# Attention operands and value differences kept in DRAM as high and low parts, and a head's two half results stored apart, in a decoder block

## The chip, the cores and the metric

The kernel runs on one core of a Trainium2 chip. The metric is the device time of one execution in microseconds (us); less is better. The times before are of three runs, and one more execution was profiled.

## The reference, cut to what matters

A decoder block over 1024 rows of 1024 values in float32: a norm, one wide input projection, two mixers side by side (stick-breaking attention of 8 heads of 64, and a gated linear attention, GLA, of 4 heads), each with its own projection and gate, an output projection, and a gated feed-forward part with a convolution of width 3 (2816 channels).

```python
proj = xn @ w_in      # sb q,k,v | GLA q,k,v,r,a | two gates
z = einsum('bhqd,bhkd->bhqk', qb, kb) * scale
log_keep = where(strict, log_sigmoid(-z), 0.0)
tail = cumsum(log_keep, reverse=True) - log_keep
w = where(strict, exp(log_sigmoid(z) + tail), 0.0)
o_sb = einsum('bhqk,bhkd->bhqd', w, vb)
y = sigmoid(gate_sb + b0) * (o_sb @ w_branch_sb) + sigmoid(gate_gla + b1) * (o_gla @ w_branch_gla)
h = h + y @ w_out
h = h + conv_ffn(rms_norm(h), ...)
```

## The kernel before, in words

Every matrix product is made of fp32r operands: a float32 value is split into a high part (a cast on ScalarE, ACT) and a low part (a subtraction on VectorE, DVE), and `mac` (L196) adds three products, high by high, high by low and low by high. So TensorE (PE) is fed by splits: `split` is a cast (L119) and a subtraction (L110). All products of the two big projections go through an Strassen-like scheme (`fast` steps), whose operands are sums of quarters.

The program runs through these stages:

- 0 to 114 us: norm, transposes, and the value projections. The last of these (`value`, L367) makes the GLA values, in a loop of 8 steps (i). In the same loop `sums` makes sums of the quarters on DVE (L110, L116) with their splits, and `differences(i)` subtracts each value row from the one before it: two loads (L439, L444), a POOL subtraction (L445), a POOL-issued store of 256 KB to `dv_d` (L446).
- 114 to 316 us: ten pairs of `fast` products (L196), some 20 us of PE each. `project_pairs` loads weights (L172, 2 loads of 512 KB a pair on the queue of SyncE, SP), splits them and adds the results on DVE (L116). `keep` finishes a pair: the eight tiles of attention queries and keys (128x1024) are stored to `sqk_d` from the POOL queue (L535).
- 316 to 545 us: attention, `attend`: four head pairs j, in each four steps tp and two heads e. `weigh` makes scores (L664), a sigmoid on ACT (L666), a mask on POOL (`affine_select`, L668) and a scan on DVE (L671). `turn_weights` transposes (L678) and splits, `gather` multiplies with the value differences (L687), whose stationary tile holds high and low part side by side (`vt`, 128 columns), so that the result has two halves of 64 partitions: ACT takes the lower one with a bias (L692), DVE adds the upper one (L116, 64x256), and SP stores 64 KB to `osb_d` (L695). `weigh` runs ahead of `gather` by up to six chunks (`AHEAD`) or 12 blocks. Between, `fill(gate_steps, 1)` puts products of the gates (L196, L568) on PE.
- `keys(j)` loads three pieces for each of two halves (256 KB each, L584, L586, SP) and splits them (ACT L590, DVE L110 64x1024), `queries(j, th)` loads two (L599) and splits them (ACT L602, DVE L110 128x1024), `value_blocks` loads 256 KB of `dv_d` for each block (L653) and splits it, `whole21` loads a quarter of the input back (`x21_d`, in rows `x_d`; L610, two loads of 1 MB) and rounds it with four casts (L614). All these loads are on SP. Their instructions are set between the chunks by generators (`coming`, `again`).
- 545 to 618 us: GLA (`gated`, L781 to L854) with the first branch projection: `osb_d` is loaded back in eight tiles of 128x512 (L955), each split by L119 and L110, and multiplied by `w_branch_sb`. The order in which `first_branch` and `gated` alternate is set by the counters `GLA`.
- 618 to 1411 us: second branch, output projection, the feed-forward part. The diff touches nothing here.

Tiles come from rings: `t8` 16 buffers, `t4` 14, `t2` 11, PSUM banks 8. A load whose buffer is still read waits in its queue, and so does all that stands behind it in that queue. The order of instructions on each engine is that of the recorded program.

Of the kernel before, what the change touches and what calls it, by code (L numbers as in the profile page):

```python
# [17 lines left out]
P = 128  # L18
# [27 lines left out]
EVERY = 1  # L46
# [19 lines left out]
def block_kernel(ctx: ExitStack, tc: tile.TileContext, x, norm_mix_g, w_in, b_gate, w_alpha_up, b_alpha,  # L66
# [32 lines left out]
    def dram(name, rows, cols):  # L99
        return dp.tile([rows, cols], F32, tag=name, name=name)  # L100
# [55 lines left out]
    dv_d = dram("dv_d", S, SBH * SBD)  # L156
    sqk_d, gr_d = dram("sqk_d", 2 * SBH * SBD, S), dram("gr_d", GH * GV, S)
    qd_d, ki_d, kt_d = (dram(n, GH * GK, S) for n in ("qd_d", "ki_d", "kt_d"))
    gate_d, ga_d = dram("gate_d", 2 * D, S), dram("ga_d", 2 * RANK, S)
    osb_d = dram("osb_d", SBH * SBD, S)  # L160
    x21_d = dram("x21_d", 2 * P, 2 * D)
# [270 lines left out]
    for n, v in enumerate(xq["21"]):  # L432
        nc.gpsimd.dma_start(by(x21_d[n * P:(n + 1) * P, :], 4), v.bitcast(F32))

    def differences(i):
# [10 lines left out]
        nc.gpsimd.dma_start(dv_d[rows, :], a)  # L446

    xsums = sums(xq)
    for i in range(NT):
        differences(i)  # L450
        fill(xsums, 2)
        value(ws2, (i + 4) % NT, gv_d)
# [68 lines left out]
    def keep(pair):  # L521
        def finish(*os):
# [3 lines left out]
            for o, (_, dst, r0) in zip(os, pair):  # L526
# [4 lines left out]
                if dst is gate_d:  # L531
# [46 lines left out]
    def keys(j, t):  # L578

        kk, raw = by(t8(), 2), t4()  # L580
# [12 lines left out]

    def queries(j, th, t):
# [687 lines left out]
```

## Time and profile before

| | |
|---|---|
| time, median of 3 runs (least to greatest) | 1412.22 us (1410.84 to 1413.24) |
| profiled execution: its own time | 1412.8 us |
| its span, granted TensorE clock | 1411.1 us, 0.994 |
| PE busy | 1385.3 us (98%) |
| PE weight load busy | 1145.4 us (81%) |
| DVE busy | 1065.4 us (76%) |
| ACT busy | 650.4 us (46%) |
| POOL busy | 111.5 us (8%) |
| bytes moved by DMA | 216.87 MB, 153 GB/s over the span |

In the rows further down, a time stands in microseconds from the start of the span, and "a<-b" is a tile written from a tile read. "x12" after a row is the number of instructions in it; a bracket behind a timeline row is the idle time of that engine before it and what ended it. A granted clock (PEclk) of 1.00 is TensorE's upper level (2.4 GHz), 0.5 its lower (1.2 GHz).

### The profile page before, as it was taken

What the parts mean: (1) busy time and instruction counts of PE and PEld (TensorE: products, weight loads), DVE (VectorE), ACT (ScalarE), POOL (GpSimd) and SP (SyncE); (2) the same over time, 40 slices, a digit from 0 to 9 for tenths busy, and PEclk for the clock granted to TensorE, in tenths of its full rate; (3) what the DMA queues carried; (4) which work ended last, traced back from release to release, by engine and by line L of the source; (5) the groups of instructions that cost most, each with busy time, mean ns of one, the idle gap of its engine ahead of it and who ended that gap; (6) DMA issues with size and microseconds to landing.
All of it is one profiled execution on the core that took longest, in us unless ns stands there. A gap on an engine that the chain in (4) does not pass through costs nothing.

```text
span 1411.1 us, 18434 instructions
## 1 busy us (share of the span) xinstructions
PE 1385.3 (98%) x6577; PEld 1145.4 (81%) x6577; DVE 1065.4 (76%) x1642; ACT 650.4 (46%) x1246; POOL 111.5 (8%) x198
## 2 busy tenths in 40 slices
PE   7999999999999999999999999999999999999997
PEld 6787888888888888878888788888888888888886
DVE  6398766767888875638446998998888977896765
ACT  6234444647766664543234543333333333454653
POOL 0040000001211110300000000100000000000000
PEclk9999999999999999999999999999999999999999
DMA  6365144276534346465324434564554437953332
GB/s 249 141 203 148 47 142 142 82 211 203 152 94 122 113 150 202 167 224 179 117 93 135 103 107 149 189 209 140 179 179 149 159 106 270 328 163 101 98 106 97
DMA packets 160188, 216.87 MB, mean 154 GB/s; under 512 B 10026, under 2 KB 103276, under 8 KB 159584
## 3 DMA queue, kind: packets, MB, share of 16 engines
q1 hardware_dynamic: 140848, 157.56, 36.5%
q0 software_dynamic: 11952, 43.58, 8.1%
q10 hardware_dynamic: 7296, 14.55, 2.8%
q8 instruction: 52, 0.85, 0.2%
q14 instruction: 40, 0.33, 0.1%
HBM read 155.75 MB, written 59.90 MB: 153 GB/s over the span
## 4 chain that ended last, share of the span: by engine, by line
PE 79%; issue 11%; DVE 6%; DMA 2%; ACT 1%; POOL 1%; POOLq 0%; ACTq 0%; DVEq 0%; SPq 0%
PE bank L196 46%; PE bank L1145 15%; PE bank L1012 5%; PE bank L367 3%; DVE t L110 3%; PE bank L687 2%; DVE t L116 2%; PE bank L664 2%; PE bank L678 2%; PE bank L320 1%; DMA gate_d<-t 1%; PE bank L427 1%; PE bank L818 1%; ACT t L119 0%; PE bank L781 0%
## 5 line engine op out<-in xcount | busy, mean ns | idle before, releaser
L196 PE MATMUL bank<-t,t 128*128 128x512 f32 x3648 | 870.6, 394 | 3.0 <-DVE t L110 2.6
L196 PEld LDWEIGHTS bank<-t,t 128*128 128x128 f32 x3648 | 682.7, 189 | 150.6 <-DVE t L110 3.8
L110 DVE TENSOR_TENSOR t<-t,t 128x512 fp32r<-128x512 f32 (+2 forms) x651 | 430.9, 696 | 82.6 <-ACT t L119 76.0
L119 ACT CAST t<-t 128x512 fp32r<-128x512 f32 x537 | 311.8, 620 | 321.5 <-DVE t L116 74.0
L116 DVE TENSOR_TENSOR t<-bank,t 128x512 f32<-128x512 f32 (+1 forms) x284 | 183.2, 655 | 119.9 <-PE bank L196 65.3
L1145 PE MATMUL bank<-t,t 128*128 128x512 f32 x924 | 209.6, 389 | 0.0
L1145 PEld LDWEIGHTS bank<-t,t 128*128 128x128 f32 x924 | 173.4, 188 | 36.0
L110 DVE TENSOR_TENSOR t<-t 128x512 f32<-128x512 f32 (+1 forms) x124 | 88.4, 721 | 5.6 <-DMA t<-in_w_ffn_in_dram 3.2
L367 PE MATMUL bank<-t,t 128*128 128x512 f32 x384 | 91.9, 398 | 0.0
L110 DVE TENSOR_TENSOR t<-bank,t 128x512 fp32r<-128x512 f32 (+4 forms) x128 | 72.2, 576 | 24.3 <-ACT t L119 23.9
L116 DVE TENSOR_TENSOR t<-t,t 128x512 f32<-128x512 f32 x107 | 76.8, 750 | 16.1 <-ACT t L487 15.4
L1012 PE MATMUL bank<-t,t 128*128 128x512 f32 x384 | 88.9, 391 | 0.0
L1043 ACT ACTIVATE t<-t,vcol 128x1024 f32<-128x1024 f32 x22 | 27.4, 1244 | 127.6 <-DVE t L116 124.0
L367 PEld LDWEIGHTS bank<-t,t 128*128 128x128 f32 x384 | 72.8, 192 | 15.6 <-DVE t L110 0.4
L1012 PEld LDWEIGHTS bank<-t,t 128*128 128x128 f32 x384 | 71.6, 188 | 14.7
L119 ACT CAST t<-bank 128x512 fp32r<-128x512 f32 (+3 forms) x124 | 61.6, 509 | 40.2 <-PE bank L320 19.7
L1045 DVE SCALAR_TENSOR_TENSOR t<-t,vcol,t 128x1023 f32<-128x1023 f32 (+1 forms) x44 | 56.3, 1279 | 14.1 <-ACT t L1043 13.9
L671 DVE TENSOR_TENSOR_SCAN t<-t,zero 128x128 f32<-128x128 f32 (+1 forms) x64 | 52.2, 823 | 16.0 <-POOL t L668 15.5
L664 PE MATMUL bank<-t,t 128*128 128x128 f32 (+3 forms) x192 | 55.5, 368 | 0.4 <-DVE t L110 0.4
L678 PE MATMUL bank<-ident,t 128*128 128x128 f32 x288 | 52.3, 274 | 0.8 <-DVE t L116 0.4
L668 POOL TENSOR_SCALAR_AFFINE_SELECT t<-t 128x128 f32<-128x128 f32 x64 | 33.3, 526 | 212.4 <-ACT t L666 199.2
L666 ACT ACTIVATE t<-bank 128x128 f32<-128x128 f32 (+3 forms) x96 | 45.7, 499 | 6.0 <-PE bank L664 4.3
(127 smaller groups left out, 773.6 us busy)
## 6 DMA issues: line engine op xcount, KB each, us to landing
t<-in_w_ffn_in_dram SPq DMA_DIRECT2D x50, 512.0 KB, 4.2
t<-in_w_in_dram SPq DMA_DIRECT2D x43, 512.0 KB, 5.3
act_d<-t POOLq DMA_DIRECT2D x22, 512.0 KB, 6.0
t<-in_w_ffn_out_dram SPq DMA_DIRECT2D x22, 512.0 KB, 7.5
wsum_d<-t POOLq DMA_DIRECT2D x22, 512.0 KB, 4.1
t<-act_d SPq DMA_DIRECT2D x22, 512.0 KB, 6.1
t<-wsum_d SPq DMA_DIRECT2D x44, 256.0 KB, 3.1
t<-sqk_d SPq DMA_DIRECT2D x40, 256.0 KB, 4.2
```

The costliest lines, as they stand in the source:

```text
L110: nc.vector.tensor_tensor(out=o, in0=a, in1=b, op=ALU.subtract)
L116: nc.vector.tensor_tensor(out=o, in0=a, in1=b, op=ALU.add)
L119: nc.scalar.copy(h, src)
L196: nc.tensor.matmul(pt, a[:, kk], b[:, kk], start=start and kk == 0 and m == 0, stop=stop and kk == k - 1 and m == 2)
L367: nc.tensor.matmul(pt, a[:, k % 4, t], b, start=k == 0 and m == 0, stop=k == NK - 1 and m == 2)
L664: nc.tensor.matmul(z[:, 0:w], q[:, a, e, ts_], kk[:, e, b0 * P:b1 * P], start=a == 0, stop=a == 1)
L666: nc.scalar.activation(ke[:, 0:w], z[:, 0:w], AF.Sigmoid, scale=-SBD ** -0.5)
L671: nc.vector.tensor_tensor_scan(out=kr, data0=kr, data1=zero.to_broadcast([P, w]), initial=1.0 if right is None else right[:, 0:1], op0=ALU ...
L678: nc.tensor.transpose(pt[:, b * P:(b + 1) * P], ke[:, b * P:(b + 1) * P], ident)
L1012: nc.tensor.matmul(pt, a[:, k % 4, t], b, start=(k == 0 and m == 0), stop=(k == NK - 1 and m == 2))
L1045: nc.vector.scalar_tensor_tensor(out=cv[:, i:], in0=av[:, :S - i], scalar=col(V_CW, (2 - i) * NF + f), in1=cv[:, i:], op0=ALU.mult, op1=AL ...
L1145: nc.tensor.matmul(pts[m][i], a[:, t], b, start=(k == 0 and x_ == 0), stop=(k == NH - 1 and x_ == 2))
```

## The change

Queries and keys are split in `keep`, when they are made, and stored as two tensors `sqkh_d` and `sqkl_d`. The value differences are split in `differences`, which moves out of the loop of value products into the loop of the `fast` steps (called at n = 0, and at odd n up to 15, so that block 0 is made twice), and stored 128x1024. Attention then loads finished parts, all from the POOL queue: `keys` four loads of 256 KB, `queries` four of 256 KB, `value_blocks` 512 KB a block, `whole21` without its casts. `gather` gives the bias to all 128 partitions and stores both halves; `osb_d` has twice the rows, and the reload before the first branch adds them. The constant `EVERY` and the import of `chain` go.

```diff
+    def dram(name, rows, cols, dt=F32):
+        return dp.tile([rows, cols], dt, tag=name, name=name)
...
-    dv_d = dram("dv_d", S, SBH * SBD)
-    sqk_d, gr_d = dram("sqk_d", 2 * SBH * SBD, S), dram("gr_d", GH * GV, S)
+    dv_d = dram("dv_d", S, SBH * 2 * SBD, F32R)
+    sqk_d = [dram(n, 2 * SBH * SBD, S, F32R) for n in ("sqkh_d", "sqkl_d")]
...
-    osb_d = dram("osb_d", SBH * SBD, S)
-    x21_d = dram("x21_d", 2 * P, 2 * D)
+    osb_d = dram("osb_d", 2 * SBH * SBD, S)
+    x21_d = dram("x21_d", 2 * P, 2 * D, F32R)
...
         nc.gpsimd.tensor_tensor(out=a, in0=a, in1=b, op=ALU.subtract)
-        nc.gpsimd.dma_start(dv_d[rows, :], a)
+        v = t4(F32R).rearrange("p (h d) -> p h d", h=SBH)
+        split(v[:, :, 0:SBD], v[:, :, SBD:P], a.rearrange("p (h d) -> p h d", h=SBH))
+        nc.gpsimd.dma_start(dv_d[rows, :], v.rearrange("p h d -> p (h d)"))
...
     for i in range(NT):
-        differences(i)
         fill(xsums, 2)
         value(ws2, (i + 4) % NT, gv_d)
...
+                if dst is sqk_d:
+                    h, l = t4(F32R), o.bitcast(F32R)
+                    split(h, l, o)
+                    for d, v in zip(dst, (h, l)):
+                        nc.gpsimd.dma_start(d[r0:r0 + P, :], v)
...
             h = slice(HALF + j * P + e * 64, HALF + j * P + e * 64 + 64)
-            nc.sync.dma_start(raw[HALVES[1 - e]], sqk_d[h, :])
-            for a in HALVES:
-                nc.sync.dma_start(kk[a, e].bitcast(F32), sqk_d[h, :])
-        for e in range(2):
-            yield
-            other = HALVES[1 - e]
-            nc.scalar.copy(kk[:, e], kk[:, e].bitcast(F32))
-            yield
-            sub(kk[other, e], raw[other], kk[other, e].bitcast(F32))
+            for a in range(2):
+                nc.gpsimd.dma_start(kk[HALVES[a], e], sqk_d[a][h, :])
...
-        for a in HALVES:
-            nc.sync.dma_start(by(q[a, 1].bitcast(F32), 2),
-                              sqk_d[j * P:(j + 1) * P, th * HALF:(th + 1) * HALF].rearrange("(e p) c -> p e c", p=64))
-        yield
-        nc.scalar.copy(q[:, 0], q[:, 1].bitcast(F32))
-        yield
-        sub(q[:, 1], q[:, 1].bitcast(F32), q[:, 0].bitcast(F32))
+        for a in range(2):
+            for r in HALVES:
+                nc.gpsimd.dma_start(by(q[r, a], 2), sqk_d[a][j * P:(j + 1) * P, th * HALF:(th + 1) * HALF].rearrange(
+                    "(e p) c -> p e c", p=64))
...
-            nc.sync.dma_start(v.bitcast(F32), by(x21_d[n * P:(n + 1) * P, :], 4))
-        yield
-        for k in range(0, 4, 2):
-            for v in q:
-                nc.scalar.copy(v[:, k:k + 2], v[:, k:k + 2].bitcast(F32))
-                yield
+            nc.gpsimd.dma_start(v, by(x21_d[n * P:(n + 1) * P, :], 4))
...
         if n > 0 and n % 2 == 0:
             fill(side, 1)
+        elif n // 2 < NT:
+            differences(n // 2)
...
-            v2 = t8().rearrange("p (b h d) -> p b h d", b=2, h=SBH)
-            for i in (len(vt), len(vt) + 1):
-                raw = t2()
-                nc.sync.dma_start(raw, dv_d[i * P:(i + 1) * P, :])
-                split(v2[:, i % 2, :, 0:SBD], v2[:, i % 2, :, SBD:P], raw.rearrange("p (h d) -> p h d", h=SBH))
-            vt.extend((v2[:, 0], v2[:, 1]))
+            v2 = by(t8(), 2)
+            for i in range(2):
+                b = len(vt) + i
+                nc.gpsimd.dma_start(v2[:, i], dv_d[b * P:(b + 1) * P, :])
+            vt.extend(by(v2[:, i], SBH) for i in range(2))
...
-            nc.scalar.activation(o[0:64, 1, c], po[64:128, c], AF.Identity,
-                                 bias=vend[:, head * NT + 2 * tp + n:head * NT + 2 * tp + n + 1])
-        add(o[0:64, 0], po[0:64, 0:2 * P], o[0:64, 1])
-        nc.sync.dma_start(osb_d[head * 64:(head + 1) * 64, tp * 2 * P:(tp + 1) * 2 * P], o[0:64, 0])
+            i = head * NT + 2 * tp + n
+            nc.scalar.activation(o[:, c], po[:, c], AF.Identity, bias=vend[:, i:i + 1])
+        for n, r in enumerate(HALVES):
+            nc.sync.dma_start(osb_d[n * HALF + head * 64:n * HALF + (head + 1) * 64, tp * 2 * P:(tp + 1) * 2 * P], o[r])
...
-            raw = t2()
-            nc.sync.dma_start(raw, osb_d[k * P:(k + 1) * P, th * HALF:(th + 1) * HALF])
-            split(*(a[:, k] for a in ob[th]), raw)
+            raws = t2(), t2()
+            for n, v in enumerate(raws):
+                nc.sync.dma_start(v, osb_d[n * HALF + k * P:n * HALF + (k + 1) * P, th * HALF:(th + 1) * HALF])
+            add(raws[0], *raws)
+            split(*(a[:, k] for a in ob[th]), raws[0])
```

The order on the engines, at the three places that matter. First POOL from the two stores of `x21_d` on, which stand ahead of the value loop (L445 is the subtraction of `differences`, `dv_d` its store). Before:

```order
L433 DMA x_d<-t_54_320 128x2048
L441 MEMSET t_106_633 1x512
L445 TENSOR_TENSOR t_106_633<-t_106_633,t_107_634 128x512
L446 DMA dv_d<-t_106_633 128x512
L445 TENSOR_TENSOR t_114_682<-t_114_682,t_115_683 128x512
L446 DMA dv_d<-t_114_682 128x512
```

and in the changed kernel (`qd_d` and `ki_d` are stores of the `fast` stage):

```order
L433 DMA x_d<-t_54_321 128x2048
L472 MEMSET t_146_962 128x128
L441 MEMSET t_158_998 1x512
L445 TENSOR_TENSOR t_158_998<-t_158_998,t_159_999 128x512
L441 MEMSET t_175_1086 1x512
L448 DMA dv_d<-t_160_1004 128x1024
L445 TENSOR_TENSOR t_175_1086<-t_175_1086,t_176_1087 128x512
L448 DMA dv_d<-t_177_1092 128x1024
L445 TENSOR_TENSOR t_204_1246<-t_204_1246,t_205_1247 128x512
L511 DMA qd_d<-t_215_1313 128x512
```

The subtractions now stand behind the memset of the `fast` stage, and two of them ahead of its first stores, instead of eight in the value loop. Second POOL at the start of attention in the changed kernel (L591 are loads of keys, L599 of queries, L646 of value differences, L606 of the input quarter, L660 the mask); before, POOL had nothing but masks here:

```order
L591 DMA t_428_2548<-sqkl_d 64x1024
L599 DMA t_439_2627<-sqkh_d 64x2x512
L646 DMA t_493_2864<-dv_d 128x1024 x2
L606 DMA t_496_2873<-x_d 128x2048
L660 AFFINE_SELECT t_443_2637<-t_443_2637 128x128
L660 AFFINE_SELECT t_445_2646<-t_445_2646 128x128
L660 AFFINE_SELECT t_452_2669<-t_452_2669 128x128
L660 AFFINE_SELECT t_456_2696<-t_456_2696 128x128
L606 DMA t_497_2874<-x_d 128x2048
L660 AFFINE_SELECT t_461_2716<-t_461_2716 128x128
L591 DMA t_529_3032<-sqkh_d 64x1024
```

The first masks now stand behind all loads of the first head pair and of three pairs of value blocks. Third DVE at the reload of `osb_d`. Before, the eight subtractions of the splits stand together (four of them shown), ahead of the GLA's copies:

```order
L110 TENSOR_TENSOR t_995_5408<-t_999_5421,t_994_5407 128x512
L110 TENSOR_TENSOR t_1001_5426<-t_1002_5427,t_1000_5425 128x512
L110 TENSOR_TENSOR t_1001_5426<-t_1003_5431,t_1000_5425 128x512
L110 TENSOR_TENSOR t_1001_5426<-t_1004_5435,t_1000_5425 128x512
L110 TENSOR_TENSOR t_1001_5426<-t_1005_5439,t_1000_5425 128x512
L788 COPY t_979_5353<-bank_5480 64x128 x2
```

and in the changed kernel, from the sixth slice on (L115 is the addition of two halves, L109 a split, L780 and L782 are the GLA's):

```order
L115 TENSOR_TENSOR t_1015_5458<-t_1015_5458,t_1016_5459 128x512
L780 COPY t_986_5365<-bank_5516 64x128 x2
L782 SCALAR_TENSOR_TENSOR t_986_5365<-t_986_5365,eend_970,bank_5539 64x128
L115 TENSOR_TENSOR t_1017_5465<-t_1017_5465,t_1018_5466 128x512
L109 TENSOR_TENSOR t_1012_5450<-t_1015_5458,t_1011_5449 128x512
L780 COPY t_987_5366<-bank_5534 64x128
L109 TENSOR_TENSOR t_1012_5450<-t_1017_5465,t_1011_5449 128x512
L115 TENSOR_TENSOR t_1019_5472<-t_1019_5472,t_1020_5473 128x512
L109 TENSOR_TENSOR t_1030_5521<-t_1021_5479,t_1030_5521 128x512
L780 COPY t_987_5366<-bank_5534 64x128
L109 TENSOR_TENSOR t_1012_5450<-t_1019_5472,t_1011_5449 128x512
```

The last additions now stand among the GLA's copies, and each waits for two loads.

## Rows read from the trace of the kernel before

**Rows 1.** The page, part 1: busy time, share of the span and instructions.

```profile
PE 1385.3 (98%) x6577; PEld 1145.4 (81%) x6577; DVE 1065.4 (76%) x1642; ACT 650.4 (46%) x1246; POOL 111.5 (8%) x198
```

**Rows 2.** What PE waited for: in total, times, longest (us).

```profile
PE bank L853 <- ACT t L847: 2.7, 2, 1.8
PE bank L196 <- DVE t L110: 2.6, 2, 1.8
```

**Rows 3.** Stretches of 50 us: busy time of each engine, PEclk, DMA share, GB/s.

```profile
100.00:150.00 50.00, 47.89 (x200) 37.73 (x199) 40.82 (x66) 22.70 (x38) 4.32 (x5) 0.97 0.43 127
350.00:400.00 50.00, 48.37 (x285) 40.97 (x285) 42.99 (x64) 38.12 (x83) 9.11 (x16) 1.00 0.52 137
850.00:900.00 50.00, 50.00 (x222) 41.40 (x221) 43.20 (x62) 18.67 (x29) 3.19 (x6) 1.00 0.58 191
```

**Rows 4.** Timeline of PE, end of the value loop: start, length, instruction, idle before.

```profile
87.63 26.68 PE L367 MATMUL bank<-t,t 128*128 128x512 f32 x117
114.15 0.61 PE L196 MATMUL bank<-t,t 128*128 128x512 f32 x2
116.54 4.57 PE L196 MATMUL bank<-t,t 128*128 128x512 f32 x12 [1.77 <-DVE t L110]
121.44 2.82 PE L196 MATMUL bank<-t,t 128*128 128x512 f32 x11 [0.34 <-ACT t L119]
```

**Rows 5.** Timeline of DVE there.

```profile
108.50 2.39 DVE L116 TENSOR_TENSOR t<-t,t 128x512 f32<-128x512 f32 x2
...
112.19 1.29 DVE L116 TENSOR_TENSOR t<-t,t 128x512 f32<-128x512 f32 x2
...
115.80 1.89 DVE L110 TENSOR_TENSOR t<-t,t 128x512 fp32r<-128x512 f32 x3
```

**Rows 6.** POOL by shape, 74 to 117 us: busy and mean ns, idle before.

```profile
L445 POOL TENSOR_TENSOR t<-t,t 128x512 f32<-128x512 f32 x8 | 13.0, 1622 | 35.9 <-DMA t<-sbv_d 33.2 <-ACT t L372 2.7
```

**Rows 7.** Stretches around the lowered clocks.

```profile
117.40:120.80 3.40, 3.40 (x10) 2.31 (x8) 3.37 (x6) 1.13 (x3) 0.00 (x0) 0.54 0.21 77
...
615.60:622.60 7.00, 5.66 (x16) 4.43 (x17) 2.59 (x5) 2.28 (x6) 0.00 (x0) 0.53 1.00 371
```

**Rows 8.** Stretches in the fast products.

```profile
183.00:203.00 20.00, 20.00 (x90) 16.56 (x89) 17.82 (x32) 8.87 (x16) 2.17 (x4) 1.00 0.44 124
203.00:223.00 20.00, 20.00 (x88) 15.83 (x87) 9.69 (x16) 8.03 (x13) 1.06 (x2) 1.00 0.48 148
```

**Rows 9.** Timeline of PE, start of attention.

```profile
353.26 0.66 PE L678 MATMUL bank<-ident,t 128*128 128x128 f32 x4 [0.36 <-ACT t L666]
...
366.76 0.33 PE L678 MATMUL bank<-ident,t 128*128 128x128 f32 x1 [0.40 <-DVE t L116]
```

**Rows 10.** Timeline of ACT there.

```profile
348.13 2.00 ACT L614 CAST t<-t 128x1024 fp32r<-128x1024 f32 x2 [0.40 <-DMA t<-x_d]
...
367.47 1.05 ACT L602 CAST t<-t 128x1024 fp32r<-128x1024 f32 x1 [3.41 <-DMA t<-sqk_d]
```

**Rows 11.** Instructions on sqk_d: ns least, median, most; its landing.

```profile
L535 POOL DMA_DIRECT2D sqk_d<-t x8: 531/538/539, 175.3 to 238.6; - x8
...
DMA to landing us min/median/max: 2.9/4.2/8.3
```

**Rows 12.** Timeline of SP at the reload of osb_d.

```profile
546.81 5.22 SPq L955 DMA_DIRECT2D t<-osb_d  x8
```

**Rows 13.** Timeline of ACT there.

```profile
554.12 2.68 ACT L119 CAST t<-t 128x512 fp32r<-128x512 f32 x4 [0.45 <-DMA t<-osb_d]
557.48 0.62 ACT L119 CAST t<-t 128x512 fp32r<-128x512 f32 x1 [0.68 <-DMA t<-osb_d]
```

**Rows 14.** Timeline of DVE there.

```profile
558.13 0.69 DVE L110 TENSOR_TENSOR t<-t,t 128x512 fp32r<-128x512 f32 x1 [0.60 <-ACT t L119]
```

**Rows 15.** Timeline of PE there.

```profile
558.91 3.35 PE L196 MATMUL bank<-t,t 128*128 128x512 f32 x13
```

**Rows 16.** A stretch of the reload.

```profile
546.00:552.00 6.00, 6.00 (x28) 4.99 (x27) 1.29 (x2) 2.38 (x5) 0.00 (x0) 1.00 0.88 281
```

More of the change, by code (lines that the diff above doesn't have):

```diff
@@ L2 @@
 from collections import deque
-from itertools import chain, islice
+from itertools import islice
 import concourse.bass as bass
@@ L45 @@
 AGAIN = 10
-EVERY = 1
 AHEAD = 6
@@ L97, in bank @@
         return ps.tile([P, HALF], F32, tag="bank", name=nm("bank"), bufs=8)
-    def dram(name, rows, cols):
-        return dp.tile([rows, cols], F32, tag=name, name=name)
+    def dram(name, rows, cols, dt=F32):
+        return dp.tile([rows, cols], dt, tag=name, name=name)
     def by(a, k):
@@ L432, in block_kernel @@
     for n, v in enumerate(xq["21"]):
-        nc.gpsimd.dma_start(by(x21_d[n * P:(n + 1) * P, :], 4), v.bitcast(F32))
+        nc.gpsimd.dma_start(by(x21_d[n * P:(n + 1) * P, :], 4), v)
     def differences(i):
@@ L530, in finish @@
                     mul(o, o, sg)
-                if dst is gate_d:
+                if dst is sqk_d:
[3 more added lines that the diff above has]
+                        nc.gpsimd.dma_start(d[r0:r0 + P, :], v)
+                elif dst is gate_d:
                     nc.scalar.activation(o, o, AF.Sigmoid, bias=col(V_BG, r0 // P))
@@ L578, in keys @@
     def keys(j, t):
-        kk, raw = by(t8(), 2), t4()
+        kk = by(t8(), 2)
         t.append(kk)
@@ L626, in block_kernel @@
             q0 = []
-            for v in (keys(0, q0), queries(0, 0, q0)):
-                fill(v, 9)
+            keys(0, q0)
+            queries(0, 0, q0)
             fill(gate_steps, 1)
@@ L631, in block_kernel @@
         del xq[a]
-    again = whole21()
     vt = []
-    vend = t2()[0:SBD, 0:SBH * NT]
+    vend = t2()[:, 0:SBH * NT]
     def last_values():
@@ L644, in last_values @@
             nc.tensor.transpose(pt[0:SBD, h * NT:(h + 1) * NT], raw[0:NT, h * SBD:(h + 1) * SBD], ident[0:NT, 0:NT])
-        nc.vector.tensor_copy(vend, pt[0:SBD, 0:SBH * NT])
+        nc.gpsimd.memset(vend[SBD:P], 0.0)
+        nc.vector.tensor_copy(vend[0:SBD], pt[0:SBD, 0:SBH * NT])
     def value_blocks(n):
         while len(vt) < n:
-            v2 = t8().rearrange("p (b h d) -> p b h d", b=2, h=SBH)
-            for i in (len(vt), len(vt) + 1):
-                raw = t2()
-                nc.sync.dma_start(raw, dv_d[i * P:(i + 1) * P, :])
-                split(v2[:, i % 2, :, 0:SBD], v2[:, i % 2, :, SBD:P], raw.rearrange("p (h d) -> p h d", h=SBH))
-            vt.extend((v2[:, 0], v2[:, 1]))
+            v2 = by(t8(), 2)
[3 more added lines that the diff above has]
+            vt.extend(by(v2[:, i], SBH) for i in range(2))
     def weigh(t, e, i, b0, b1, right):
@@ L708, in attend @@
         for j in range(SBH // 2):
-            t, nxt, coming = nxt, [], iter(())
+            t, nxt = nxt, []
             for tp in range(NT // 2):
                 if tp == 0:
-                    coming = queries(j, 1, t)
+                    queries(j, 1, t)
                 if tp == NEXT[j > 0] and j + 1 < SBH // 2:
-                    coming = chain(keys(j + 1, nxt), queries(j + 1, 0, nxt))
+                    keys(j + 1, nxt)
+                    queries(j + 1, 0, nxt)
                 for e in range(2):
@@ L727, in attend @@
                             right = weigh(t, e, i, b0, b1, right)
-                            fill(coming, 1)
                             if j == 0:
                                 chunk += 1
-                                if chunk >= AGAIN and (chunk - AGAIN) % EVERY == 0:
-                                    fill(again, 1)
+                                if chunk == AGAIN:
+                                    whole21()
                                 if chunk >= 2:
```

3 lines of the change are left out of this document (2 added, 1 removed).

## The prediction, made before the result was known

> **What bounds the kernel now.** The page's first part comes first: PE is busy 98% of the span and no other engine over 81% [rows 1]. So work that is saved on DVE or ACT is worth nothing by itself; what counts is where PE waits, or runs at the lower clock. The list of PE's waits says how little that is: after the start, 2.7 us on the GLA's end (L853) and 2.6 us on DVE's splits are the largest [rows 2]. The stretches of 50 us say where: PE loses 2.11 us from 100 to 150 and 1.63 us from 350 to 400, and nothing from 850 to 900, though DVE is busy for 43.2 us there [rows 3]. A busy DVE alone therefore does not hold PE. The change touches three places where PE waits or will wait, and I cost each.
>
> The sum is made against the profiled execution, 1412.8 us, which stands 0.6 us above the median of the runs, 1412.22; I put the difference on that median. 0.2% is 2.8 us, about what a measurement of this kernel can tell from no change: under 1409.4 is faster, over 1415.0 slower.
>
> **Place 1, the end of the value loop (114 us): a gain.** PE finishes its 117 value products at 114.3, starts two products of the first pair, and then stands 1.77 us until DVE's L110 at 115.80 is through, then 0.34 us more for a cast [rows 4, 5]. DVE is late because it never rests in this loop, and because POOL's subtractions slow it: a pair of L116 takes 2.39 us while one runs and 1.29 us without [rows 5]. There are eight of them, 1622 ns each [rows 6]: 8 x 1.1 = 8.8 us on DVE. The change takes them out. By the order two come back ahead of the first pair's splits are used up, so DVE is 6.6 to 8.8 us earlier, far more than the 1.77 + 0.34 us that PE stood. That the two loads of the first weights come earlier too is needed, and follows, since they wait for a sum on DVE and for a value product that PE does at about 98 us. Gain: 2.11 us of idle time, and 0.15 us for each of the two restarts (the 117 products follow each other at 26.68 / 117 = 0.23 us, while two take 0.61 us, so one alone 0.38). After the pause the granted clock is 0.54, the lower level, for 3.4 us [rows 7]: 3.4 x 0.46 = 1.6 us. Together 4.0 us; bounds 1.9 (the clock falls elsewhere) and 4.4.
>
> **Place 1b, the fast products: new work, covered.** Per pair of 20 us come up to two tiles of 128x1024 to split (ACT 1.05 us by the L602 row [rows 10]; DVE about 1.3 us, twice the 0.69 us of a 512-wide split [rows 14]), one split of value differences (0.62 and 0.69 us) and one POOL subtraction, which slows DVE by 1.1 us: 2 x 1.3 + 0.69 + 1.1 = 4.4 us. From 183 to 203 DVE is busy 17.82 us of 20, so it runs over by 2.2 us, but the next 20 us hold only 9.69 [rows 8]. A lag of 2.2 us is held by the splits that DVE makes a pair ahead; the 850 to 900 stretch shows that such a DVE leaves PE whole [rows 3]. If that cover were gone it would cost 2.2 us in each of the two busiest pairs. I take 0.2, bounds 0 and 4. The eight more stores of 512 KB, at 0.54 us of POOL each [rows 11], wait for nothing that PE needs soon.
>
> **Place 2, the start of attention: a gain.** From 350 to 367 PE stops four times for 0.36 to 0.5 us, on ACT and DVE [rows 9]. In front of these pauses ACT does two pairs of L614 casts of 2.00 us, and waits 3.41 us for a load of `sqk_d` ahead of an L602 cast, with the attention's own casts behind it in its queue [rows 10]. The change removes all of this: 4 casts of `whole21`, 16 casts and 16 subtractions of keys and queries, 16 of the value blocks, and 32 additions of 64x256. Gain: the 1.63 us that PE loses here [rows 3] and 4 x 0.15 for the restarts: 2.2 us, bounds 0 and 2.5. The rest of that removed work was beside a busy PE: nothing. In exchange 50 loads go to POOL's queue, with its masks (L668) behind them. An issue takes 0.54 us there, and the loads of such tiles land after 4.2 us, at most 8.3 [rows 11]. The masks behind four to six loads are 2 to 3 us later; `weigh` is six chunks ahead of `gather`, and 96 chunks in 229 us make six of them 14 us. I take nothing; what it costs if that fails is a rival.
>
> **Place 3, the reload of `osb_d`: a loss.** Before, eight loads are issued from 546.81 [rows 12]; the last four pieces land between 554.1 and 557.48, 0.84 us apart [rows 13], the last subtraction ends at 558.82 [rows 14]. PE reads the second half of the rows from the fifth of its products at 558.91 on, so from 559.8, and the eighth slice at 562.3 [rows 15]; in the changed order about a microsecond later. Slack: 3.5 to 4.5 us. Now there are sixteen loads, so eight more at 0.84 us: 6.7 us, and an addition of 0.69 us in front of the cast: 7.4 us. So PE stands 2.9 to 3.9 us in bits, as the additions come in one by one; I take 3.4. The bounds: at the 281 GB/s of this stretch [rows 16] the 2.1 MB take 7.5 us, and PE stands 4.7; at the 371 GB/s of the fullest stretch [rows 7] they take 5.7, and 1.8 are left. Behind the additions on DVE stand the GLA's copies (L780), on SP the loads of gates and branch weights, all later by the same few microseconds; they are used after the eighth slice and shift with it. And such pauses took the clock down twice in the trace, for 3.4 us after 1.77 us of idle time and for 7.0 us after 2.7 us [rows 2, 4, 7]; the four short pauses at 350 did not (PEclk 1.00 [rows 3]). I take the smaller, 1.6 us, bounds 0 and 3.3.
>
> **The sum.** -4.0 + 0.2 - 2.2 + 3.4 + 1.6 = -1.0 us: 1411.8 for a profiled execution, and **1411.2 us** on the median. That is no change that can be told. The ends: -4.4 - 2.5 + 1.8 = -5.1 gives 1407.1, and -1.9 + 4 + 0 + 4.7 + 3.3 = +10.1 gives 1422.3.
>
> **The rivals.**
>
> *Faster: the reload leaves the clock alone.* If the additions come in so evenly that PE never stands over a microsecond at a time, the 1.6 us go, and with transfers at the faster rate 1.6 us of the pause too: -1.0 - 3.2 = -4.2, so 1408.0, and down to 1406 if the pauses were hidden further. For it: eight pieces that come one by one; the short pauses at 350 did not lower the clock. Against it: the sum of the pauses, above that of 114 us.
>
> *Slower: POOL's queue becomes attention's bound.* Here the masks wait behind loads, and each load behind its buffer and the landings before it. If a head pair's eight to twelve loads come in two rounds of the greatest landing, 2 x 8.3 = 16.6 us [rows 11], the masks are later than the 14 us of lead, and PE stands the difference, 2.6 us, at each of three changes of j: -1.0 + 7.8 = +6.8, so 1419.0. It decides as soon as a mask starts over 14 us after its sigmoid. Against it: the loads are issued early, and the median landing is half of that.
> The Trainium skill speaks for this rival: its page "SBUF — State Buffer", section "SBUF: two separate sides", says that a DMA issued from GpSimd has its descriptors written by that engine's cores, that these are locked out while DVE runs an operation in a 2-port mode, and advises the SP or ACT queue. By that rule each load on POOL would start later under such a DVE operation, and this case could come true. The trace does not show it so far: POOL's eight stores of queries and keys, issued while DVE was at work and split weights, took 531 to 539 ns each [rows 11].
>
> *No gain at place 1.* If the two subtractions that fall ahead of the first pair, or the loads, keep the splits late, the 4.0 us stay: -1.0 + 4.0 = +3.0, so 1415.2. For it: DVE is as full as before up to 112 us. Against it: 6.6 us of room.
>
> **How the numbers follow.** The forecast has a chance of 0.46 (its own range 1409.4 to 1414); the faster rival 0.37, the POOL rival 0.09, no gain at place 1 0.08. Half of the last counts as the same, half as slower, and 0.02 of the forecast's bounds lie beyond 1415. That makes faster 0.37, same 0.48, slower 0.15. The range from 1406.0 to 1416.0 holds the forecast, most of the faster rival, and the place 1 case; the POOL rival and the tails are left out.
>
> **What would show it.** Right: in the changed profile PE goes from value products to the first pair without a pause at 114 us and at a clock of 1.00; ACT and DVE have idle time from 340 to 370 and PE's pauses there are gone; a new wait of PE on DVE (L109, behind L115) of about 3.4 us stands some 6 us earlier than the same work before, near 553 to 562, with the clock down after it. Wrong: a pause at 114 that remains (place 1), waits on the masks or scans in attention (POOL's queue), PE whole at the reload (a faster result), or waits on DVE between 120 and 300 (place 1b).

## The result, and the profile after

| | before | changed |
|---|---|---|
| median (least to greatest) | 1412.20 us (1410.84 to 1413.24, 6 runs) | 1421.43 us (1420.29 to 1424.42, 6 runs) |
| ratio, 95% interval | | 1.0069 [1.0056, 1.0082] |
| profiled execution, its span, clock | 1412.8, 1411.1, 0.994 | 1422.37, 1420.7, 0.992 |

The change makes the kernel 9.2 us slower. The forecast was 1411.2, no change, in a range to 1416.0: it is wrong, and the time lies outside.

The page's first part, as in [rows 1]:

```profile
PE 1387.1 (98%) x6577; PEld 1146.3 (81%) x6577; DVE 1045.4 (74%) x1611; ACT 638.0 (45%) x1237; POOL 145.2 (10%) x268
```

DVE is busy 20 us less and ACT 12 us less, PE is busy 1.8 us more with the same instructions, and the span is 9.6 us longer. So most of the time is in PE's waits, and their list (answering to [rows 2]) has changed:

```profile
PE bank L196 <- DVE t L109: 7.8, 7, 2.5
PE bank L196 <- ACT t L118: 6.8, 2, 6.2
PE bank L845 <- ACT t L839: 2.7, 2, 1.8
```

Before, PE waited 2.6 us for DVE and next to nothing for ACT in its products of L196; now 7.8 and 6.8 us. The end of the GLA (L845, formerly L853) is the same. Taken by place:

**The end of the value loop** (timeline of PE, answering to [rows 4]):

```profile
85.70 27.82 PE L367 MATMUL bank<-t,t 128*128 128x512 f32 x122
113.35 11.95 PE L196 MATMUL bank<-t,t 128*128 128x512 f32 x52
```

The first pair's products follow the value products without a pause, 0.8 us earlier than before, and the clock does not fall: the stretch from 100 to 150 us, which lost 2.11 us [rows 3], is full.

```profile
100.00:150.00 50.00, 50.00 (x219) 40.60 (x218) 34.90 (x60) 22.05 (x38) 5.21 (x7) 1.00 0.49 144
350.00:400.00 50.00, 50.00 (x300) 43.41 (x300) 35.33 (x51) 27.98 (x69) 12.97 (x27) 1.00 0.54 132
```

The second row is **the start of attention**: its small pauses of 1.63 us [rows 3] are gone as well.

**The fast products** (waits of PE from 130 to 310 us; there were none before):

```profile
PE bank L196 <- DVE t L109: 3.5, 4, 1.5
PE bank L196 <- ACT t L118: 0.6, 1, 0.6
```

Five pauses, 4.1 us. The longest, on the timeline of PE:

```profile
236.21 9.14 PE L196 MATMUL bank<-t,t 128*128 128x512 f32 x39 [1.53 <-DVE t L109]
```

It lasts from 234.68 to 236.21, and DVE works without a break from 227.59 on: it is behind. The largest hold-up in the 30 us before is a stand of ACT, with the casts that DVE's splits need behind it:

```profile
214.45 2.19 ACT L118 CAST t<-t 128x512 fp32r<-128x512 f32 x4 [7.39 <-POOL t L445]
```

DVE:

```profile
215.10 1.29 DVE L109 TENSOR_TENSOR t<-t,t 128x512 fp32r<-128x512 f32 x2 [4.31 <-ACT t L118]
```

ACT stands 7.39 us for POOL's subtraction: its next instruction is a cast of value differences, and the casts of weights stand behind it. This comes with nearly every block. What ACT, DVE and POOL waited for from 120 to 310 us (total, times, longest):

```profile
ACT t L118 <- POOL t L445: 43.8, 8, 11.8
```

DVE:

```profile
DVE t L109 <- ACT t L118: 35.4, 15, 8.8
```

POOL:

```profile
POOL t L445 <- DMA t<-sbv_d: 85.3, 8, 13.9
```

The kernel before has no wait of ACT for POOL there. POOL in turn stands for the loads of `sbv_d`, which stand on SP behind loads of weights (here the issue of three of them runs over 22.84 us):

```profile
207.67 22.84 SPq L172 DMA_DIRECT2D t<-in_w_in_dram  x3
230.56 0.58 SPq L439 DMA_DIRECT2D t<-sbv_d  x1
```

Those loads of weights wait in their turn for DVE, from 120 to 310 us:

```profile
SPq L172 <- DVE t L109: 130.1, 10, 20.7
```

SP waited for DVE before as well (142.6 us), but now the waits run in a circle: DVE for ACT, ACT for POOL, POOL for SP and SP for DVE.

**Ahead of the first value sums** (timelines of ACT and PE):

```profile
336.73 1.14 ACT L118 CAST t<-t 128x512 fp32r<-128x512 f32 x2 [10.84 <-DMA t<-in_w_in_dram]
```

PE:

```profile
337.40 0.79 PE L196 MATMUL bank<-t,t 128*128 128x512 f32 x1 [6.24 <-ACT t L118]
```

PE stands 6.24 us, its longest pause after the start, for the cast of a gate's weights, which waits 10.84 us for their load on SP. No row of before has such a wait. The stretch from 305 to 335 us, of the kernel before and of the changed one, and the landing of weight loads issued from 285 to 345 us, again of both:

```profile
305.00:335.00 30.00, 29.91 (x150) 24.57 (x149) 22.12 (x34) 15.80 (x33) 3.78 (x8) 1.00 0.69 189
```

The changed kernel:

```profile
305.00:335.00 30.00, 26.17 (x127) 21.32 (x125) 9.57 (x17) 5.73 (x11) 8.42 (x18) 0.99 1.18 362
```

Landing before:

```profile
DMA to landing us min/median/max: 3.8/5.3/6.4
```

Landing in the changed kernel:

```profile
DMA to landing us min/median/max: 4.5/25.2/25.5
```

The transfers went from 189 to 362 GB/s and the DMA share from 0.69 to 1.18; the median load of 512 KB, which landed after 5.3 us, takes 25.2. What moved there is POOL's (its loads of value blocks and of the input quarter, with their landing):

```profile
L646 POOL DMA_DIRECT2D t<-dv_d x6: 537/538/584, 308.2 to 314.9; - x6
...
DMA to landing us min/median/max: 9.7/11.6/14.2
```

The quarter:

```profile
L606 POOL DMA_DIRECT2D t<-x_d x2: 537/546/555, 316.3 to 322.0; - x2
...
DMA to landing us min/median/max: 15.0/15.6/16.3
```

Six value blocks of 512 KB and the quarter's two loads of 1 MB are all issued from 308.2 to 322.0 us. Before, the blocks had half the bytes and stood on SP between the weights from 305.9 to 336.2, and the quarter was issued at 337.2.

**The reload of `osb_d`** (timelines of PE and DVE, and two stretches):

```profile
567.71 0.96 PE L196 MATMUL bank<-t,t 128*128 128x512 f32 x3 [0.97 <-DVE t L109]
...
573.20 5.00 PE L196 MATMUL bank<-t,t 128*128 128x512 f32 x14 [2.54 <-DVE t L109]
```

DVE:

```profile
571.85 0.69 DVE L115 TENSOR_TENSOR t<-t,t 128x512 f32<-128x512 f32 x1 [1.91 <-DMA t<-osb_d]
```

The stretches:

```profile
568.00:574.00 6.00, 3.46 (x14) 2.56 (x14) 4.03 (x10) 2.05 (x4) 0.37 (x1) 0.92 0.86 267
574.00:580.00 6.00, 6.00 (x33) 4.54 (x33) 5.68 (x13) 2.00 (x4) 2.30 (x5) 0.79 1.07 380
```

Two pauses, 3.51 us together, behind additions (L115) that wait for their loads, and 6 x 0.08 + 6 x 0.21 = 1.7 us lost to the clock. The split that ends the longer pause, and the sixteen loads on SP:

```profile
572.46 0.69 DVE L109 TENSOR_TENSOR t<-t,t 128x512 fp32r<-128x512 f32 x1
```

SP:

```profile
553.33 14.11 SPq L948 DMA_DIRECT2D t<-osb_d  x16
```

By DVE's order, shown with the change, this split is that of the sixth slice: it stands behind the addition of the seventh, which is the one that waits 1.91 us for its load.

### The profile page after: what moved, and what is told of

It is laid out like the page before. It is cut to its first block, busy times and chain, and to the rows that moved or that the text cites. A ratio compares the mean times of both kernels' runs of the same rounds, so it can differ in the third digit from the quotient of the medians.

```text
span 1420.7 us, 18501 instructions
## 1 busy us (share of the span) xinstructions
PE 1387.1 (98%) x6577; PEld 1146.3 (81%) x6577; DVE 1045.4 (74%) x1611; ACT 638.0 (45%) x1237; POOL 145.2 (10%) x268
## 4 chain that ended last, share of the span: by engine, by line
PE 81%; DMA 7%; DVE 6%; ACT 3%; issue 2%; SPq 1%; POOL 1%; POOLq 0%; ACTq 0%; DVEq 0%
PE bank L196 44%; PE bank L1139 15%; PE bank L367 6%; PE bank L1006 5%; DVE t L109 3%; DMA t<-sbv_d 3%; PE bank L679 3%; PE bank L656 2%; PE bank L670 2%; DMA t<-in_w_in_dram 2%; DVE t L115 2%; ACT t L118 1%; DMA gate_d<-t 1%; PE bank L320 1%; DMA dv_d<-t 1%
## 5 line engine op out<-in xcount | busy, mean ns | idle before, releaser
L196 PE MATMUL bank<-t,t 128*128 128x512 f32 x3648 | 875.2, 395 | 14.8 <-DVE t L109 7.8
L196 PEld LDWEIGHTS bank<-t,t 128*128 128x128 f32 x3648 | 683.5, 189 | 165.5 <-DVE t L109 12.5
L109 DVE TENSOR_TENSOR t<-t,t 128x512 fp32r<-128x512 f32 (+2 forms) x652 | 430.6, 694 | 131.8 <-ACT t L118 125.4
L118 ACT CAST t<-t 128x512 fp32r<-128x512 f32 (+1 forms) x546 | 319.6, 626 | 361.8 <-DVE t L109 76.1
L115 DVE TENSOR_TENSOR t<-bank,t 128x512 f32<-128x512 f32 x252 | 169.9, 685 | 74.4 <-PE bank L1006 37.4
L109 DVE TENSOR_TENSOR t<-bank,t 128x512 fp32r<-128x512 f32 (+4 forms) x128 | 72.5, 580 | 41.8 <-ACT t L118 40.2
L115 DVE TENSOR_TENSOR t<-t,t 128x512 f32<-128x512 f32 x115 | 75.6, 687 | 9.8 <-ACT t L488 5.3
L109 DVE TENSOR_TENSOR t<-t 128x512 f32<-128x512 f32 x116 | 79.5, 693 | 3.8 <-DMA t<-in_w_ffn_in_dram 3.3
L663 DVE TENSOR_TENSOR_SCAN t<-t,t,zero 128x512 f32<-128x512 f32 x32 | 41.0, 1283 | 14.7 <-ACT t L658 13.4
```

Of the source, the lines that this page charges most:

```text
L109: nc.vector.tensor_tensor(out=o, in0=a, in1=b, op=ALU.subtract)
L115: nc.vector.tensor_tensor(out=o, in0=a, in1=b, op=ALU.add)
L118: nc.scalar.copy(h, src)
L196: nc.tensor.matmul(pt, a[:, kk], b[:, kk], start=start and kk == 0 and m == 0, stop=stop and kk == k - 1 and m == 2)
L663: nc.vector.tensor_tensor_scan(out=kr, data0=kr, data1=zero.to_broadcast([P, w]), initial=1.0 if right is None else right[:, 0:1], op0=ALU ...
```

## The experiments

Each was timed against the kernel before on its own chip in the same rounds, and its ratio is to that.

| kernel | median us | ratio to before, 95% interval |
|---|---|---|
| the change | 1421.43 | 1.0069 [1.0056, 1.0082] |
| before, differences moved | 1407.47 | 0.9962 [0.9949, 0.9975] |
| change, halves added in `gather` | 1415.15 | 1.0022 [1.0012, 1.0031] |
| change, rows of 512 bytes | 1424.29 | 1.0089 [1.0072, 1.0105] |
| change, loads on SP | 1429.84 | 1.0125 [1.0110, 1.0140] |
| change, quarter held | 1414.63 | 1.0020 [1.0011, 1.0030] |
| change, quarter and blocks held | 1417.54 | 1.0036 [1.0023, 1.0048] |
| change, differences unsplit | 1416.73 | 1.0037 [1.0024, 1.0050] |
| change, queries and keys unsplit | 1425.37 | 1.0096 [1.0075, 1.0116] |
| change, halves in `gather`, quarter held | 1408.04 | 0.9970 [0.9956, 0.9984] |
| the same, differences unsplit | 1406.71 | 0.9970 [0.9956, 0.9984] |
| before, differences moved, quarter held | 1411.75 | 0.9999 [0.9987, 1.0012] |
| change, halves in `gather`, quarter held, split a step later | 1402.99 | 0.9935 [0.9921, 0.9949] |

My theory after the trace: three separate losses (pauses in the fast products, the burst of POOL's loads, the reload), and one gain at 114 us. The rivals were that the move itself costs something, that the transfers just lack bandwidth, or that one loss hides another.

**The move alone.** The kernel before, with this edit:

```diff
     for i in range(NT):
-        differences(i)
         fill(xsums, 2)
...
+        elif n // 2 < NT:
+            differences(n // 2)
```

> The kernel before with one thing moved: the value differences are made in the loop of the fast products, unsplit and stored as before. If the gain at the end of the value loop is real and the subtractions cost nothing where they go: no pause of PE at 114 us, and 1412.2 - 4.0 = about 1408 us. Rival: the loads and subtractions by themselves make the splits of the fast products late (new waits of PE between 140 and 290 us, some 5 us): 1410 to 1413 us.

Measured 1407.47 us, a gain of 4.4 by the medians (the interval of the ratio allows 3.5 to 7.2). The list of PE's waits has no pause at 114 us and none up to 310 us. Loads and POOL's subtractions cost nothing there, so the pauses of the change come from what it adds to the move.

**The reload undone.** The changed kernel with `gather`, `osb_d` and its reload as before:

```diff
-    osb_d = dram("osb_d", 2 * SBH * SBD, S)
+    osb_d = dram("osb_d", SBH * SBD, S)
...
+        add(o[0:64, 0], po[0:64, 0:2 * P], o[0:64, 1])
+        nc.sync.dma_start(osb_d[head * 64:(head + 1) * 64, tp * 2 * P:(tp + 1) * 2 * P], o[0:64, 0])
...
-            raws = t2(), t2()
...
-            add(raws[0], *raws)
```

> The changed kernel with the addition of a head's two halves back in the attention, and the reload of eight tiles as before. If the reload costs what its two waits show (3.5 us) and the lower clock after them (about 1.6 us): 1421.4 - 5 = about 1416.5 us, and no wait of PE at the reload. Rival: the two waits were slack that another wait takes (the end of the GLA): 1420 to 1422 us.

1415.15 us: 6.3 less than the change, at the reload no wait of PE is left, and no other took its place. The 32 additions of 64x256 go back to DVE in attention and cost nothing there.

**Which theory of the burst.** The same transfers in short rows:

```diff
-    dv_d = dram("dv_d", S, SBH * 2 * SBD, F32R)
+    dv_d = dp.tile([S, SBH, 160], F32R, tag="dv_d", name="dv_d")
...
-    x21_d = dram("x21_d", 2 * P, 2 * D, F32R)
+    x21_d = dp.tile([2 * P, 16, 160], F32R, tag="x21_d", name="x21_d")
```

> The changed kernel with the value differences and the input quarter kept in DRAM in padded rows, so that the same bytes move on the same queue at the same place, in runs of 512 bytes instead of 4 and 8 KB. If the load of the gates' weights (runs of 512 bytes, SP) is starved because POOL's long runs take turns with it one for one: its landing comes down from about 22 us to under 10, PE's wait of 6.2 us at 331 us is under 1.5 us, and the time about 1414 us. Rival, plain lack of bandwidth: the bytes are the same, the wait stays at 4 to 7 us, and the time at 1420 to 1422 us.

Half of it came: the weights land twice as fast and PE's wait for them is gone, but the quarter is late now and the time did not fall: 1424.29 us. The blocks and the quarter were issued within a microsecond or two of the same times (309.1 to 322.8 us). Landing of weights and of the quarter, the stretch, and PE's waits from 310 to 360 us:

```profile
DMA to landing us min/median/max: 4.5/12.7/14.2
```

The quarter:

```profile
DMA to landing us min/median/max: 25.2/25.2/25.3
```

The stretch:

```profile
305.00:335.00 30.00, 30.00 (x147) 24.82 (x146) 13.78 (x22) 11.34 (x24) 14.63 (x24) 1.00 1.52 309
```

The waits:

```profile
PE bank L656 <- DVE t L109: 3.1, 1, 3.1
PE bank L679 <- DVE t L109: 1.3, 2, 0.8
PE bank L670 <- DVE t L109: 0.6, 1, 0.6
```

So the length of the rows does bear on how the transfers are shared out. But the total came down from 362 to 309 GB/s, and other waits of 5.0 us appeared. Sharing is part of it; that so much was asked for at once is the other part, which the runs with held loads test.

**One queue.** The loads of blocks and quarter on SP:

```diff
-            nc.gpsimd.dma_start(v, by(x21_d[n * P:(n + 1) * P, :], 4))
+            nc.sync.dma_start(v.bitcast(F32), by(x21_d[n * P:(n + 1) * P, :], 4).bitcast(F32))
...
-                nc.gpsimd.dma_start(v2[:, i], dv_d[b * P:(b + 1) * P, :])
+                nc.sync.dma_start(v2[:, i].bitcast(F32), dv_d[b * P:(b + 1) * P, :].bitcast(F32))
```

> The changed kernel with the loads of value differences and of the input quarter on SP's queue, in front of and between the weights' loads, in the same long rows. If it is the turns between two queues that starve the weights: one queue, so a weight load lands some 2 to 6 us after what stands ahead of it, PE's wait at 331 us is under 2 us, 1414 to 1416 us. Rival, plain lack of bandwidth: the wait stays at 4 to 7 us and the time at 1420 to 1422 us.

A miss, and neither theory's number: 1429.84 us, with PE's waits from 300 to 350 us and the weights' landing:

```profile
PE bank L196 <- ACT t L118: 11.5, 2, 7.1
```

The weights' loads and their landing:

```profile
L172 SPq DMA_DIRECT2D t<-in_w_in_dram x4: 384/764/7081, 306.5 to 326.4; - x4
...
DMA to landing us min/median/max: 10.7/18.1/22.5
```

In one queue the weights stand behind the blocks at the issue as well (one issue took 7.1 us). Counted from their issue they land somewhat sooner, after 18.1 us instead of 25.2, but PE waits for them twice, the second time until 346.5 us, where the changed kernel's wait ended at 337.4. So turns between the two queues are not needed for the weights to be late.

**The burst taken apart.** The quarter's loads made to wait for the scan of the tenth chunk, by a one-element write of that scan's result into the tile ahead of the load:

```diff
-    def whole21():
+    def whole21(held):
         q = quarter()
+        for v in q:
+            nc.vector.tensor_copy(v[0:1, 0, 0:1], held[0:1, 0:1])
...
-                                    whole21()
+                                    whole21(right)
```

> The changed kernel with the two loads of the input quarter (2 MB) held back until the scan of the tenth chunk, about where they were issued before (a one-element write by DVE into the tile makes them wait). If the burst of POOL's loads at 308 to 335 us is what delays the gates' weights: 2 MB less in front of them, at the 300 KB a microsecond that POOL's queue had, is some 6 us, so PE's wait at 331 us (6.2 us) is 0 to 1 us, and the time about 1414 us. Rival: the value blocks (3 MB, ahead of the quarter) are enough to delay them: the wait stays at over 4 us, 1419 to 1422 us.

1414.63 us, 6.8 less than the change. The quarter is issued at 339.6 us instead of 316.3, and the 6.2 us are gone (PE's waits from 310 to 345 us; landing of the weights):

```profile
PE bank L681 <- DVE t L109: 0.4, 1, 0.4
```

The landing:

```profile
DMA to landing us min/median/max: 4.4/17.3/18.3
```

The weights still take 17.3 us, but PE does not wait for them any more. Holding the blocks too:

```diff
             v2 = by(t8(), 2)
+            for i in range(2):
+                nc.vector.tensor_copy(v2[0:1, i, 0:1], held[0:1, 0:1])
```

> As the kernel with the quarter held back, with the loads of the value blocks held in the same way until the scan of the chunk that asks for them. Burst theory: no wait of PE on the gates' weights, DMA share under 1 from 310 to 330 us, 1413 to 1415 us. Rival: held loads come too late for the first sums with the values (L679), and a wait there takes the place of the one removed: 1417 us or more.

1417.54 us, the rival's time: no wait on weights, but the quarter now lands late, as the rival had it of the blocks (and the DMA share from 310 to 330 us is 1.02, not under 1):

```profile
PE bank L196 <- DMA t<-x_d: 2.7, 1, 2.7
```

**The pauses in the fast products.** Value differences stored whole, and loaded on SP and split, as before, but made in the fast products; then queries and keys stored whole instead, also loaded on SP. The first:

```diff
-        split(v[:, :, 0:SBD], v[:, :, SBD:P], a.rearrange("p (h d) -> p h d", h=SBH))
-        nc.gpsimd.dma_start(dv_d[rows, :], v.rearrange("p h d -> p (h d)"))
+        nc.gpsimd.dma_start(dv_d[rows, :], a)
...
+                split(v2[:, i % 2, :, 0:SBD], v2[:, i % 2, :, SBD:P], raw.rearrange("p (h d) -> p h d", h=SBH))
```

> The changed kernel with the value differences stored whole and split when they are loaded, as before, but still made in the loop of the fast products. If the new pauses between 150 and 290 us (waits of 3.5 + 0.6 us, some 6 us in all with their restarts) come from the splits of value differences, which hold ACT and DVE until POOL's subtraction is through: they go, and with half the bytes of value blocks the wait at 331 us is shorter too: 1411 to 1415 us. Rival: they come from the splits of queries and keys: the pauses stay, and only the part at 331 us changes: 1417 us or more.

The second:

```diff
-                if dst is sqk_d:
-                    h, l = t4(F32R), o.bitcast(F32R)
-                    split(h, l, o)
-                    for d, v in zip(dst, (h, l)):
-                        nc.gpsimd.dma_start(d[r0:r0 + P, :], v)
...
+            nc.scalar.copy(kk[:, e], kk[:, e].bitcast(F32))
...
+            sub(kk[other, e], raw[other], kk[other, e].bitcast(F32))
...
+        nc.scalar.copy(q[:, 0], q[:, 1].bitcast(F32))
...
+        sub(q[:, 1], q[:, 1].bitcast(F32), q[:, 0].bitcast(F32))
```

> The changed kernel with queries and keys kept whole and split in attention, as before. If the pauses between 150 and 290 us come from these splits (eight casts of 1.05 us and eight subtractions of 1.2 us): they go, about 1415 us. Rival, the splits of value differences: the pauses stay, the small pauses of the attention's start come back (+2), and the time is 1420 us or more.

Both took pauses away, and both missed their times (1416.73 us against 1411 to 1415, 1425.37 against about 1415). Without the splits of differences none is left from 120 to 310 us. Without those of queries and keys one is left, at 154 us, ahead of where the first such tile is split:

```profile
PE bank L196 <- DVE t L109: 0.7, 1, 0.7
```

So either kind by itself fits, all but for one pause, and it needs both for the rest. The times were missed in attention: with unsplit differences PE waits in attention for scans and value splits (L669 and L678, 5.3 us), without split queries and keys 9.9 us for the weights, before 345 us. I had not separated two things that the splits do: they load DVE, and the casts wait for POOL in ACT's queue. The last run does.

**Repairs together.** The addition back in `gather` and the quarter held, the two edits above in one kernel:

> The changed kernel with both repairs, the addition back in attention and the quarter's loads held. If the reload (6.3 us by the run with the addition back) and the burst (6.8 us by the run with the quarter held) are separate losses, they add: 1421.4 - 13.1 = about 1408 us, with only the pauses from 150 to 290 us left. Rival: removing one uncovers a wait of the other's work: 1411 us or more.

1408.04 us: the two losses add, 13.4 us together where 6.3 and 6.8 make 13.1. With the differences unsplit in addition, by the edit above:

> As the kernel with both repairs, and the value differences stored whole and split when loaded (but made in the loop of the fast products). If the pauses from 150 to 290 us come from the splits of value differences on top of those of queries and keys, some 6 us go: 1402 to 1404 us, faster than both kernels. Rival: the splits in attention bring back the waits seen there with unsplit differences (L669, L678, some 5 us): 1407 to 1410 us.

1406.71 us, a little under the rival's range, and the ratio is that of the run with both repairs (0.9970), so no gain is shown: the pauses went, and waits in attention (3.6 us) came, as the rival had it. And the kernel before with only the move and the quarter without casts, its loads held:

```diff
+        for v in q:
+            nc.vector.tensor_copy(v[0:1, 0, 0:1], held[0:1, 0:1])
         for n, v in enumerate(q):
-            nc.sync.dma_start(v.bitcast(F32), by(x21_d[n * P:(n + 1) * P, :], 4))
-        yield
-        for k in range(0, 4, 2):
-            for v in q:
-                nc.scalar.copy(v[:, k:k + 2], v[:, k:k + 2].bitcast(F32))
-                yield
+            nc.gpsimd.dma_start(v, by(x21_d[n * P:(n + 1) * P, :], 4))
```

> The kernel before with two parts of the change: the value differences made in the loop of the fast products, unsplit, and the input quarter stored rounded and loaded without casts, its loads held as above. If ACT's four casts of 1.05 us were what made the small pauses at the start of attention: 1407.5 - 2 = 1405 to 1406 us. Rival: the pauses there come from the splits of queries and keys: 1407 to 1408 us.

A miss: 1411.75 us, since here the held quarter comes too late (PE's waits from 345 to 375 us), so it says nothing on the casts:

```profile
PE bank L196 <- DMA t<-x_d: 4.0, 1, 4.0
```

**The split a step later.** Both repairs, and the cast and subtraction of value differences put some 10 us behind POOL's subtraction:

```diff
         nc.gpsimd.tensor_tensor(out=a, in0=a, in1=b, op=ALU.subtract)
+        yield
         v = t4(F32R).rearrange("p (h d) -> p h d", h=SBH)
...
+    made = iter(())
...
-        if n > 0 and n % 2 == 0:
-            fill(side, 1)
+        if n % 2 == 0:
+            fill(side, n > 0)
+            fill(made, 1)
         elif n // 2 < NT:
-            differences(n // 2)
+            fill(made, 1)
+            made = differences(n // 2)
+            fill(made, 1)
```

> The kernel with both repairs (1408.0 us), in which the value differences are split one step of the fast products (some 10 us) after POOL's subtraction has been issued, and block 0 is made once. If the pauses from 150 to 290 us come from ACT and DVE standing in their queues for POOL's subtraction and its loads: they go, and some 5 to 6 us with them, about 1402 to 1403 us. Rival, plain load of DVE by the splits of both kinds: the pauses from 220 to 290 us stay, and the time is 1406 to 1408 us.

1402.99 us, ratio 0.9935 [0.9921, 0.9949]: faster than both kernels, and 5.05 under the run without this edit. No pause is left from 120 to 310 us. The list of PE's waits, whole but for the start:

```profile
PE bank L851 <- ACT t L845: 2.7, 2, 1.8
PE bank L196 <- DVE t L109: 0.8, 1, 0.8
PE bank L196 <- DMA t<-x_d: 0.3, 1, 0.3
```

The splits are all there, one of nine fewer, and the waits in line are mostly gone. What ACT and DVE waited for from 120 to 310 us:

```profile
ACT t L118 <- POOL t L445: 11.2, 1, 11.2
```

DVE:

```profile
DVE t L109 <- ACT t L118: 15.8, 8, 6.8
```

And the stretch with the longest pause, of the changed kernel and of this one:

```profile
223.00:243.00 20.00, 18.46 (x81) 14.64 (x80) 16.09 (x28) 13.17 (x22) 3.30 (x4) 1.00 0.61 202
```

This run:

```profile
223.00:243.00 20.00, 20.00 (x90) 16.58 (x89) 19.82 (x31) 11.25 (x18) 6.10 (x8) 1.00 0.72 229
```

DVE is fuller here than in the changed kernel, 19.82 us of 20, and PE has no pause. So the pauses came from the standing in line, not from the load of DVE: the queues of ACT and DVE were held for POOL's subtraction. That the splits of queries and keys had used up the lead that would have covered it fits the two runs above and was not tested further. (The edit also moves the splits to another place among the other work, and what the ninth split was worth by itself was not tried.)

## Why the prediction was wrong

- **Place 1** was right: -4.0 forecast, -4.4 by the move alone; the pause at 114 us and the lower clock behind it are gone, as named.
- **Place 1b** is the first step that failed: "a lag of 2.2 us is held by the splits that DVE makes a pair ahead ... I take 0.2". It cost 5.05 us by the run with the later split, over the upper bound of 4. I counted the splits as DVE time only, and by that count DVE had room: with the later split it was busy 19.8 of 20 us from 223 to 243 and PE lost nothing. What I left out is the wait that the change adds, 43.8 us of it, on ACT, for POOL's subtraction, for loads behind SP's weights, with the weights' casts and DVE's subtractions queued behind it. Such a wait costs what stands behind it in the queue, and no sum of busy times shows it. The sign was the one that I had named for place 1b: waits on DVE between 120 and 300.
- **Place 2** was half right. The pauses of 1.63 us went; which of the removed work had made them is not shown, nor is the 0.6 us for the restarts. But "in exchange 50 loads go to POOL's queue ... I take nothing" was the second step that failed: 6.8 us. I priced the issue and the masks behind it, and took the landing times of before, 4.2 and at most 8.3 us, for loads that now all start together. The quarter's loads had been held at 337 us by SP's queue; on POOL's nothing held them. Blocks of twice the bytes and the quarter filled the transfers from 308 us, and the loads that stayed on SP were the ones to be late. The POOL rival had the right change of queue and the wrong victim: no mask or scan in the list of PE's waits, but the weights.
- What stood beside that rival on the page "SBUF — State Buffer" of the Trainium skill, section "SBUF: two separate sides" (that loads issued from GpSimd are held while DVE runs certain operations), these runs do not show: POOL's issues of value blocks took 537 to 584 ns, and its loads landed after 11.6 us where SP's took 25.2. Whether any DVE operation beside them was of that kind, no row says.
- **Place 3** was right in kind, PE waiting for DVE behind late additions, and met its size partly by luck: 3.4 us of pauses forecast and 3.51 measured, 1.6 for the clock and 1.7 measured. But the last split of the reload ended 22.9 us after the first load's issue (553.33 to 576.19), against 12.0 before, so 10.8 later where I had 7.4; and the longer pause was for the sixth slice, held on DVE behind the seventh's addition. So the slack was larger than I had it too, and the two errors came out even. By the run without it the reload cost 6.3; part of the rest may be the clock at the end of the GLA, which held in that run's profile.
- The sum in place of mine: -4.4 + 5.05 + (6.8 - 2.2) + 6.3 = +11.5, against 9.2 measured. The 2.3 us too many are of the size of what the clock gives or takes from one execution to the next (below); I did not settle them.

## What to carry to other kernels

Moving a load to another queue also takes away what paced it: ask when each moved load will now start, sum the bytes of all that start together, and look which small load that PE needs soon will share the transfers with them. A split put right behind a slow producer on another engine holds the whole queue; put a step later, the same work cost PE nothing here. Where work is made once instead of often, the part that is read back at a stage's very end (here the reload of halves) pays double bytes on the critical path, so add before storing.

## What was not expected of the hardware

Under a full load, the queue with the longer rows got the larger share: weights in runs of 512 bytes landed after 25.2 us beside rows of 4 and 8 KB, and after 12.7 beside the same bytes in runs of 512, while the quarter went from 15.6 to 25.2 us.

And the end of the GLA has the same wait of 2.7 us in all these kernels, but the granted clock behind it was 0.53 for 7.0 us in the profile of the kernel before [rows 7] and stayed at 1.00 in that of the kernel with the halves added back and the quarter held (a stretch of 10 us with the wait in it, and the next):

```profile
610.00:620.00 10.00, 7.32 (x45) 5.45 (x44) 4.05 (x8) 5.98 (x28) 0.00 (x0) 1.00 0.92 312
620.00:630.00 10.00, 10.00 (x46) 8.28 (x45) 2.46 (x4) 0.00 (x0) 0.00 (x0) 1.00 0.86 294
```

That is some 3 us that no edit of mine was aimed at, and it need not be the kernel's doing. Six executions of this kernel fall into two groups: three of 1407.1 to 1407.4 us with a mean granted clock of 0.999, the profiled one among them, and three of 1408.7 to 1409.9 us with 0.996 or 0.997. So a difference of 2 us between two medians can be the clock alone. Where in the program the second group lost it, and why the clock held in the first, stays open.
